# Fixing GpSimd's order in an attention layer, and moving the steps that scale its weights

## The chip, the cores and the metric

The kernel runs on one core of a Trainium2 chip. The metric is the device time of one execution, in microseconds. TensorE multiplies, VectorE and ScalarE work element by element and move results out of TensorE's accumulators (PSUM), GpSimd works element by element on SBUF, and SyncE issues the DMAs. Each engine takes its instructions in one fixed order, which is decided when the program is compiled.

## The reference, cut to what matters

A trunk of two layers runs over 512 prompt rows and 32 sample rows (544 columns here, since the kernel holds activations transposed). Layer 0 mixes tokens with an RWKV-7 recurrence. Layer 1, the only one that the change touches, is differential attention. Its input projection is one wide product:

```
h = rmsnorm(x, norm_w)
q, k, v, qm, gate = jnp.split(h @ w_in, [MIX_W, 2 * MIX_W, 3 * MIX_W, 3 * MIX_W + MEM_W], axis=-1)
...
attn = probs(q1, k1) - lam * probs(q2, k2)
o = rmsnorm(jnp.einsum('bhqk,bkhd->bqhd', attn, v), subln) * (1.0 - lam_init)
out = jnp.concatenate([o, mem_attention(qm, mk, mv)], axis=-1) * jax.nn.silu(gate)
return x + out @ w_out, k, v
```

There are 12 heads of width 128, four heads of attention to a memory of 256 rows, and a gate of 2048 columns. All is in float32, so the kernel makes each large product from parts.

## The kernel before, in words

**Blocks.** Layer 1's input projection is cut into 56 blocks of 128 output columns: for each head its values, keys and queries, then gates, and for four heads a memory query and a memory gate. `steps` (line 461) multiplies one block: two halves of 272 columns, eight contraction tiles in each, three matmuls to a tile, so 48 matmuls or steps, numbered 0 to 47. The three matmuls are high weight times high activation, high weight times low activation, and low weight times high activation. The first use of a block's low part is therefore its third matmul (step 2), and of the second half of that low part its fifteenth (step 14). After each half an evacuation moves the result out of PSUM: one ScalarE instruction for values, keys and memory queries, ScalarE and then VectorE for gates, and for queries two ScalarE and two VectorE instructions that take turns.

**Preparing a block's weights.** Raw weights are float32 and come by DMA into one of four buffers (`load_pair`, line 316; tile `h16s` in the profile). They are split into two float16 parts. First a power of two is found that brings them into float16's range: ScalarE squares all 1024 elements of a partition and adds them up (`square_total`, line 326; the squares themselves are thrown away into a tile `junkw`); TensorE adds the partitions with a matrix of ones (`total_spread`, line 336, a matmul with one column); VectorE makes the scale from the sum (`scales`, two small instructions). Then `split_scaled` (line 366) makes the parts, in halves of 512 elements: ScalarE writes the high part `whs` (raw times scale, rounded), GpSimd multiplies raw by the scale in place (line 374), GpSimd subtracts the high part and writes the low part `wls` (line 375). A last small GpSimd instruction (`inverse`, line 346, and for memory queries a second one) makes the inverse scale, with which the evacuation multiplies.

**Buffers.** `whs` has two buffers. `wls` has two buffers as well, under the tag "wlo", and from the fourth block on the discarded squares `junkw` take one of the same two (line 333). Which tile gets which buffer is decided by the compiler, in an order that it works out beforehand; a tile's buffer is free again when the last instruction that uses the tile is done.

**The order around the change.** `stream` (line 1879) runs the 56 blocks and places the preparation between matmuls. During block b it issues the split of block b+1 at the steps of SPLITS1 (two for `whs`, two for the scaling, two for the subtraction, one for the inverse), the load of block b+4 at the steps of LOADS1 (1 and 14), the squares of block b+3 at step 10 (STAT1), their sum over partitions at step 46 (SPREAD1, into a spare column of the second half's PSUM bank) and the scale in the next block at step 8 (SCALE1). `diff_layer` (line 1939) adds the attention of earlier heads at written-out places between the same matmuls: scores, exponentials, transposes, stores, weighted sums, memory attention.

**Queues.** In this stage TensorE, VectorE, ScalarE and SyncE are wrapped in `Queue` (line 124): while `self.ordered` is set, each instruction is tied behind the one issued before it on its engine, so that the order written in the code is the order that runs. GpSimd is not wrapped: its instructions are issued through `nc.gpsimd`, and the compiler chooses their order. The inverse is one that it moves: written as the last of the split, it runs right after the VectorE instruction that makes its scale. GpSimd's other work in this stage is the low part of the keys (`keys`, line 2010, two instructions per head) and one small product per gate (line 1993).

Of the kernel before, what the change touches and what calls it, by code (L numbers as in the profile page):

```python
# [18 lines left out]
P = 128  # L19
# [20 lines left out]
TILES1 = ((156,178),(188,210),(220,244),(254,280))  # L40
MEMAT1 = (60, 80, 180, 276, 294, 306, 324, 330, 346, 362, 402, 420, 484, 552)
MEMAT1B = MEMAT1[:10] + (400, 430, 490, 590)
LOADS1, SPLITS1 = (1, 14), (2, 5, 9, 13, 17, 20, 23)
STAT1, SPREAD1, SCALE1 = 10, 46, 8
EXP = float(1 << 23)
ROOT = float(0x5F3759DF) + 14 * EXP
SAMPLE1 = ((310, "s"), (338, "m"), (362, "t"), (386, "w"), (406, "n"), (464, "r"))
# [87 lines left out]
class Trunk:  # L135
# [187 lines left out]
            self.se.dma_start(raw[:, q * h : q * h + h], src[q * h * P : (q + 1) * h * P, c0 : c0 + P].rearrange("(k p) c -> p k c", p=P))  # L323
            yield

    def square_total(self, rec):

        rec["st"] = st = self.sts[rec["n"] % 4]
        with self.nc.allow_low_precision("a bound, rounded before a power of two is taken from it"):
            if rec["n"] < 3:  # L330
                junk = self.raws[3].bitcast(BF16)[:, :, :P]
            else:
                junk = self.wp.tile([P, KT, P], BF16, tag="wlo", name="junkw", bufs=2)[:]
            self.ae.activation(junk, rec["raw"], AF.Square, accum_out=st)

    def total_spread(self, rec, out, start):

        rec["sum"] = out
        self.te.matmul(out, self.ones16, rec["st"], start=start, stop=True, skip_group_check=not start)

    def scales(self, rec):

        rec["s"] = self.scale[:, rec["n"] : rec["n"] + 1]
        self.power(rec["s"], rec["sum"])

    def inverse(self, inv, rec):

        gp, kind = self.nc.gpsimd, rec["kind"]
        gp.tensor_scalar(inv.bitcast(I32), rec["s"].bitcast(I32), -1.0, self.cx[:, kind % 4 : kind % 4 + 1], ALU.mult, ALU.add)
        if kind == 4:  # L350
            gp.tensor_scalar(inv, inv, P ** -0.5, None, ALU.mult)

    def power(self, s, total):

# [3 lines left out]
    def measured(self, rec):  # L358

        if "s" not in rec:  # L360
            self.square_total(rec)
            ps = self.psx.tile([P, 512], F32, tag="x", name="ps_st")
            self.total_spread(rec, ps[:, 0:1], True)
            self.scales(rec)

    def split_scaled(self, rec):

        hi = self.wp.tile([P, KT, P], F16, tag="whi", name="whs", bufs=2)
        lo = self.wp.tile([P, KT, P], F16, tag="wlo", name="wls", bufs=2)
        raw, s = rec["raw"], rec["s"]  # L370
        ks = [slice(q * KT // 2, (q + 1) * KT // 2) for q in range(2)]
        gp = self.nc.gpsimd
        todo = [(lambda k=k: self.ae.activation(hi[:, k], raw[:, k], AF.Copy, scale=s), 0.0) for k in ks]
        todo += [(lambda k=k: gp.tensor_scalar(raw[:, k], raw[:, k], s, 1.0, ALU.mult, ALU.mult), 0.0) for k in ks]  # L374
        todo += [(lambda k=k: gp.tensor_tensor(lo[:, k], raw[:, k], hi[:, k], ALU.subtract), 0.0) for k in ks]  # L375
        inv = self.unscale[:, rec["n"] : rec["n"] + 1]
        todo.append((lambda: self.inverse(inv, rec), 0.0))
        return (hi, lo, inv), todo

    def weights(self, src, c0):  # L380

# [19 lines left out]
    def split(self, raw):  # L401

        if isinstance(raw, dict):
            return self.split_scaled(raw)
        third = self.third is not None and self.turn % 3 == 2
        self.turn += 1
        p, n = (self.third, 1) if third else (self.wp, 2)
        hi = p.tile([P, KT, P], F32R, tag="whi", name="whi", bufs=n)
        lo = p.tile([P, KT, P], F32R, tag="wlo", name="wlo", bufs=n)
        todo = []  # L410
        for q in range(2):
            k = slice(q * KT // 2, (q + 1) * KT // 2)
            todo.append((lambda k=k, q=q: self.ae.copy(hi[:, k], raw[q][:]), 0.0))
            low = self.nc.gpsimd if self.inner else self.ve
            todo.append((lambda k=k, q=q: low.tensor_tensor(lo[:, k], raw[q][:], hi[:, k].bitcast(F32), ALU.subtract), LATER))
        return (hi, lo), todo

# [43 lines left out]
    def steps(self, w, evac):  # L461

        n = 0
        for v in (slice(0, TH), slice(TH, T)):
            if len(self.open) > 1:
                self.until(self.open.pop(0))
            ps = self.psg.tile([P, 512], F32, tag="g", name="ps_g")
            for k in range(KT):
                for t, x in ((0, self.hh), (0, self.hl), (1, self.hh)):
                    self.te.matmul(ps[:, :TH], w[t][:, k, :], x[:, k, v], start=k == 0 and x is self.hh and t == 0,  # L470
                                             stop=k == KT - 1 and t == 1)
                    if k == KT - 1 and t == 1:
                        self.open.append(evac(ps[:, :TH], v))
                    yield
                    n += 1
                    if n == SPREAD1 and self.rec is not None:
                        self.total_spread(self.rec, ps[:, 2 * TH - 64 : 2 * TH - 63], False)

    @staticmethod
    def two(ap):  # L480
# [1269 lines left out]
    def scaled_pool(self):  # L1750

        nc, p = self.nc, self.h0
        self.hh, self.hl = (lambda t: (t[:, 0], t[:, 1]))(p.tile([P, 2, KT, T], F16, tag="hh", name="h16"))
        part = p.tile([P, KT * T], F32, tag="hl", name="h16s")
        self.raws = [part[:, i * D : i * D + D].rearrange("p (k c) -> p k c", c=P) for i in range(4)]
        at = 4 * D

        def small(n):
            nonlocal at
            at += n  # L1760
            return part[:, at - n : at]

        self.scale, self.unscale, self.ones16 = small(56), small(56), small(P // 2).bitcast(BF16)
        nc.gpsimd.memset(self.ones16, 1.0)
        self.sts = [small(1).bitcast(BF16)[:, 0:1] for _ in range(4)]
        self.subg = small(DH)
        self.nscaled = 0
        sq, st, sx, self.nwx, self.cx = small(KT), small(1).bitcast(BF16)[:, 0:1], small(1), small(KT), small(4)
        with nc.allow_low_precision("a bound, rounded before a power of two is taken from it"):
            self.ae.activation(sq, self.nw[1], AF.Square, accum_out=st)  # L1770
        ps = self.psx.tile([P, 512], F32, tag="x", name="ps_nw")
        self.te.matmul(ps[:, 0:1], self.ones16, st, start=True, stop=True)
        self.power(sx, ps[:, 0:1])
        self.ve.tensor_scalar(sx, sx, 2.0 ** -4, None, ALU.mult)
        self.ve.tensor_scalar(self.nwx, self.nw[1], sx, None, ALU.mult)
        for n in range(4):
            self.ve.tensor_scalar(self.cx[:, n : n + 1], sx.bitcast(I32), -1.0, (381.0 - n) * EXP, ALU.mult, ALU.add)
# [101 lines left out]
    def stream(self, makes):  # L1879
# [3 lines left out]
                return self.made.pop(0), []  # L1883
            return self.split(self.early.pop(0))

        cur = nxt()
        for make in makes:
            w, todo = cur
            for fn, _ in todo:
                fn()  # L1890
            cur = nxt()
            todo = cur[1]
            last = self.rec
            self.rec = next((x for x in self.early if isinstance(x, dict) and "st" not in x), None)
            raws = self.load_steps(*self.ahead.pop(0)) if len(self.early) < (3 if isinstance(self.early[0], dict) else 2) else iter(())
            for i, _ in enumerate(make(w)):
                yield
                if i in LOADS1:
                    next(raws, None)
                if i in SPLITS1 and todo:  # L1900
                    todo.pop(0)[0]()
                if i == SCALE1 and last is not None:
                    self.scales(last)
                if i == STAT1 and self.rec is not None:
                    self.square_total(self.rec)
        for fn, _ in cur[1]:
            fn()
        self.made.append(cur[0])
# [30 lines left out]
    def diff_layer(self, dq, p, mp, mctx, pool_early, order, made):  # L1939
# [50 lines left out]
        def make_gate(g):  # L1990
            def make(w):
                half[g] = w[2]
                nc.gpsimd.tensor_scalar(subg[:, g : g + 1], self.subs, w[2], None, ALU.mult)
                yield from self.steps(w, self.gate_evac(self.o1[g], w[2])[2])
            return make

# [13 lines left out]
        def keys(st):  # L2010
            k, h = st["k"], st["h"]
            st["kh"] = kh = dq.tile([P, 2, T], F32R, tag="kh", name="kh", bufs=QB)
            for m in range(2):
                hi = kh[rows[m], m, :]
                self.ae.copy(hi, k[rows[m], :])
                nc.gpsimd.tensor_tensor(self.kz[h % 2][rows[m], m, :], k[rows[m], :], hi.bitcast(F32), ALU.subtract)
            self.ae.copy(st["G"]["ks"][:, st["j"], :], k[:, TP:])
            st["kout"] = turn_out(k, 0, st["G"]["scr"][0][:, st["j"], :])

# [325 lines left out]
    def run(self):  # L2345
# [7 lines left out]
        self.ordered, self.later, self.open = False, [], []  # L2353
        self.place_no = self.acted = 0
        nc = self.nc
        self.te, self.ve, self.ae, self.se = (Queue(self, e) for e in (nc.tensor, nc.vector, nc.scalar, nc.sync))
        self.c = self.pool("const", 1)
        self.hctx = ExitStack()
        hp = self.pool("h", 1, ctx=self.hctx, side="right")
# [60 lines left out]
```

## Time and profile before

| what | value |
|---|---|
| median of the runs | 1400.07 us |
| runs | 1396.4, 1400.07, 1400.42 us |
| profiled execution, its own time | 1406.7 us |
| its span, from first to last instruction | 1404.5 us |
| attention layer's 56 blocks, first matmul to end | 826.8 to 1275.2 us of the span |

The profile is of one execution. A row of a group gives the line of the code (132 is the line of the helper that issues all queued instructions), the engine, the operation, what it writes and reads, the shape and the count; then the busy time, the mean duration in ns, and the time that the engine stood idle just before, with what ended it. In the timeline the columns are start, duration, and the same names; the bracket at the end is the idle time before and its releaser, where "issue" stands for a wait that the profile could not put down to one. PEld is TensorE's weight load, a suffix q (POOLq, SPq) an engine's sequencer.

### The profile page before, as it was taken

How to read it: one execution, taken by the hardware profiler on the slowest of the kernel's cores; microseconds unless marked ns; L12 is line 12 of the kernel's file. 1: busy time of each engine (PE TensorE's matmuls, PEld its weight loads, DVE VectorE, ACT ScalarE, POOL GpSimd, SP SyncE). 2: the span in 40 equal slices, each digit the busy share in tenths (PEclk: the TensorE clock that was granted, in tenths of full speed). 3: DMA queues.
4: the chain of work that ended last, by engine and by line, in shares of the span. 5: the costliest groups of instructions: out<-in, count | busy, mean ns of one | idle time of the engine just before them, and what ended most of it. 6: DMA issues, size and time to landing. Idle time of an engine off the chain costs nothing. (4 is left out here: it accounts for less than half of the span.)

```text
span 1404.5 us, 31863 instructions
## 1 busy us (share of the span) xinstructions
PE 1315.7 (94%) x11657; PEld 1197.3 (85%) x11657; DVE 907.9 (65%) x2319; ACT 852.7 (61%) x2204; POOL 646.2 (46%) x1175
## 2 busy tenths in 40 slices
PE   6999999999999999899999999989999898999797
PEld 6998899999999999898899987868777776778797
DVE  7766777788778777766763545545774567756343
ACT  7665677777776777565553357656655675763221
POOL 2227576556755585620120077555554655561000
PEclk9999999999999999999999999999999999999898
DMA  7552223332233323333384447756776667666421
GB/s 241 177 137 56 61 55 93 84 76 68 73 84 79 77 62 80 79 86 121 108 258 127 130 128 170 155 142 160 170 167 132 154 139 179 147 155 194 148 68 64
DMA packets 418295, 171.51 MB, mean 122 GB/s; under 512 B 195210, under 2 KB 402579, under 8 KB 418139
## 3 DMA queue, kind: packets, MB, share of 16 engines
q1 hardware_dynamic: 417994, 168.96, 46.5%
q8 instruction: 92, 1.51, 0.5%
q14 instruction: 65, 0.52, 0.1%
q10 hardware_dynamic: 144, 0.52, 0.1%
HBM read 130.84 MB, written 41.92 MB: 123 GB/s over the span
## 5 line engine op out<-in xcount | busy, mean ns | idle before, releaser
L132 PE MATMUL ps_g<-h,whs 128*128 128x272 f16 x1792 | 329.1, 283 | 0.0
L132 PE MATMUL ps_g<-hl,whi 128*128 128x272 f32 x976 | 284.3, 297 | 0.6 <-POOL hl L581 0.5
L132 PE MATMUL ps_g<-hh,wlo 128*128 128x272 f32 x912 | 277.6, 304 | 1.3 <-DVE wlo L132 1.3
L132 PE MATMUL ps_g<-hh,whi 128*128 128x272 f32 x912 | 275.0, 302 | 0.9 <-ACT hh L132 0.9
L132 PE MATMUL ps_g<-h,wls 128*128 128x272 f16 x896 | 254.1, 284 | 17.8 <-POOL wls L375 17.7
L870 POOL TENSOR_TENSOR tm<-u,m 102x84 f32<-102x84 f32 (+23 forms) x372 | 158.1, 425 | 166.1 <-DMA m<-sc 138.0
L132 PEld LDWEIGHTS <-whs 128*128 128x128 f16 x1792 | 176.5, 99 | 38.6 <-issue 4.8
L132 DVE TENSOR_TENSOR wlo<-raw,whi 128x512 fp32r<-128x512 f32 x208 | 148.7, 730 | 83.7 <-ACT whi L132 82.4
L132 PEld LDWEIGHTS ps_g<-hl,whi 128*128 128x128 f32 x976 | 184.1, 191 | 2.4 <-POOL hl L581 0.7
L132 ACT CAST whi<-raw 128x512 fp32r<-128x512 f32 x210 | 125.3, 616 | 98.1 <-PE ps_g L132 44.5
L132 PEld LDWEIGHTS ps_g<-hh,whi 128*128 128x128 f32 x912 | 174.7, 192 | 4.4 <-ACT hh L132 1.3
L132 PEld LDWEIGHTS ps_g<-hh,wlo 128*128 128x128 f32 x912 | 174.2, 191 | 4.8 <-DVE wlo L132 2.1
L872 POOL TENSOR_TENSOR u<-u,tm 102x84 f32<-102x84 f32 (+23 forms) x372 | 159.1, 428 | 29.1
L132 PE MATMUL ps_g<-hi,whi 128*128 128x272 f32 x448 | 130.7, 292 | 11.0 <-ACT hi L132 11.0
L375 POOL TENSOR_TENSOR wls<-h16s,whs 128x512 f16<-128x512 f32 x112 | 128.1, 1164 | 18.7 <-issue 9.8
L132 PE MATMUL ps_g<-lo,whi 128*128 128x272 f32 x448 | 130.9, 292 | 0.9 <-DVE lo L132 0.9
L132 PE MATMUL ps_g<-hi,wlo 128*128 128x272 f32 x448 | 130.3, 291 | 0.2 <-DVE wlo L132 0.2
L132 PEld LDWEIGHTS <-wls 128*128 128x128 f16 x896 | 88.7, 99 | 41.4 <-POOL wls L375 21.6
L374 POOL TENSOR_SCALAR h16s<-h16s 128x512 f32<-128x512 f32 x112 | 78.9, 714 | 50.9 <-ACT whs L132 49.6
L132 PEld LDWEIGHTS ps_g<-hi,whi 128*128 128x128 f32 x448 | 85.6, 191 | 11.3 <-ACT hi L132 11.2
L132 PEld LDWEIGHTS ps_g<-lo,whi 128*128 128x128 f32 x448 | 85.5, 191 | 1.8 <-DVE lo L132 1.8
L132 PEld LDWEIGHTS ps_g<-hi,wlo 128*128 128x128 f32 x448 | 85.7, 191 | 0.4 <-DVE wlo L132 0.4
(423 smaller groups left out, 2941.2 us busy)
## 6 DMA issues: line engine op xcount, KB each, us to landing
raw<-in_rw_in_dram SPq DMA_DIRECT2D x114, 256.0 KB
h16s<-in_df_in_dram SPq DMA_DIRECT2D x112, 256.0 KB
raw<-in_w_out_dram SPq DMA_DIRECT2D x64, 256.0 KB
ptr<-pk SPq DMA_DIRECT2D x44, 160.0 KB
aT<-ptr SPq DMA_DIRECT2D x11, 640.0 KB
scr<-sg SPq DMA_DIRECT2D x96, 68.0 KB
out_dram<-scr SPq DMA_DIRECT2D x6, 1024.0 KB
m<-sc SPq DMA_DIRECT2D x36, 128.0 KB
```

The costliest lines, as they stand in the source:

```text
L132: return lambda *a, **k: self.trunk.tie(self, issue(*a, **k))
L374: todo += [(lambda k=k: gp.tensor_scalar(raw[:, k], raw[:, k], s, 1.0, ALU.mult, ALU.mult), 0.0) for k in ks]
L375: todo += [(lambda k=k: gp.tensor_tensor(lo[:, k], raw[:, k], hi[:, k], ALU.subtract), 0.0) for k in ks]
L870: nc.gpsimd.tensor_tensor(tm[:, :n, :wd], u3[:, :n, kx : kx + 1].to_broadcast(sh), m3[:, kx : kx + 1, kx + 1 :].to_broadcast(sh), ALU.mult)
L872: nc.gpsimd.tensor_tensor(u3[:, :n, kx + 1 :], u3[:, :n, kx + 1 :], tm[:, :n, :wd], ALU.add)
```

## The change

GpSimd gets a `Queue` of its own (`self.ge`) and the attention layer's GpSimd instructions go through it. The inverse scale is made by VectorE, right behind the scale, and so is the product per gate. The squares are made in two halves of 512 elements, at steps 11 and 27, each with its own sum; the discarded tile is taken at the first half and dropped after the second. The sum over partitions (now two matmuls, one for each half's sum, accumulating in one column) moves to step 12 of the next block, and scale and inverse to step 20 there. The split's places move from steps 2, 5, 9, 13, 17, 20 to 2, 5, 7, 9, 12, 15; its seventh place, the inverse's, is gone.

```diff
-LOADS1, SPLITS1 = (1, 14), (2, 5, 9, 13, 17, 20, 23)
-STAT1, SPREAD1, SCALE1 = 10, 46, 8
+LOADS1, SPLITS1 = (1, 14), (2, 5, 7, 9, 12, 15)
+STAT1, SPREAD1, SCALE1 = (11, 27), 12, 20
...
-    def square_total(self, rec):
-
-        rec["st"] = st = self.sts[rec["n"] % 4]
+    def square_total(self, rec, q):
+
+        if q == 0:
+            rec["st"] = self.sts[rec["n"] % 4]
+            if rec["n"] < 3:
+                rec["junk"] = self.raws[3].bitcast(BF16)[:, :, :P]
+            else:
+                rec["junk"] = self.wp.tile([P, KT, P], BF16, tag="wlo", name="junkw", bufs=2)[:]
+        k = slice(q * KT // 2, (q + 1) * KT // 2)
         with self.nc.allow_low_precision("a bound, rounded before a power of two is taken from it"):
-            if rec["n"] < 3:
-                junk = self.raws[3].bitcast(BF16)[:, :, :P]
-            else:
-                junk = self.wp.tile([P, KT, P], BF16, tag="wlo", name="junkw", bufs=2)[:]
-            self.ae.activation(junk, rec["raw"], AF.Square, accum_out=st)
+            self.ae.activation(rec["junk"][:, k], rec["raw"][:, k], AF.Square, accum_out=rec["st"][:, q : q + 1])
+        if q:
+            del rec["junk"]
 
     def total_spread(self, rec, out, start):
 
         rec["sum"] = out
-        self.te.matmul(out, self.ones16, rec["st"], start=start, stop=True, skip_group_check=not start)
+        for q in range(2):
+            self.te.matmul(out, self.ones16, rec["st"][:, q : q + 1], start=start and q == 0, stop=True,
+                           skip_group_check=not (start and q == 0))
 
     def scales(self, rec):
 
-        rec["s"] = self.scale[:, rec["n"] : rec["n"] + 1]
-        self.power(rec["s"], rec["sum"])
-
-    def inverse(self, inv, rec):
-
-        gp, kind = self.nc.gpsimd, rec["kind"]
-        gp.tensor_scalar(inv.bitcast(I32), rec["s"].bitcast(I32), -1.0, self.cx[:, kind % 4 : kind % 4 + 1], ALU.mult, ALU.add)
+        rec["s"], rec["inv"] = (t[:, rec["n"] : rec["n"] + 1] for t in (self.scale, self.unscale))
+        self.power(rec["s"], rec.pop("sum"))
+        kind, inv = rec["kind"], rec["inv"]
+        self.ve.tensor_scalar(inv.bitcast(I32), rec["s"].bitcast(I32), -1.0, self.cx[:, kind % 4 : kind % 4 + 1], ALU.mult, ALU.add)
         if kind == 4:
-            gp.tensor_scalar(inv, inv, P ** -0.5, None, ALU.mult)
+            self.ve.tensor_scalar(inv, inv, P ** -0.5, None, ALU.mult)
...
-        gp = self.nc.gpsimd
+        gp = self.ge
...
-        inv = self.unscale[:, rec["n"] : rec["n"] + 1]
-        todo.append((lambda: self.inverse(inv, rec), 0.0))
-        return (hi, lo, inv), todo
+        return (hi, lo, rec["inv"]), todo
...
                     if n == SPREAD1 and self.rec is not None:
-                        self.total_spread(self.rec, ps[:, 2 * TH - 64 : 2 * TH - 63], False)
+                        self.total_spread(self.rec, ps[:, 480:481], False)
...
-        cur = nxt()
+        cur, rec = nxt(), None
...
-            last = self.rec
-            self.rec = next((x for x in self.early if isinstance(x, dict) and "st" not in x), None)
+            self.rec, rec = rec, next((x for x in self.early if isinstance(x, dict) and "st" not in x), None)
...
-                if i == SCALE1 and last is not None:
-                    self.scales(last)
-                if i == STAT1 and self.rec is not None:
-                    self.square_total(self.rec)
+                if i == SCALE1 and self.rec is not None:
+                    self.scales(self.rec)
+                if i in STAT1 and rec is not None:
+                    self.square_total(rec, STAT1.index(i))
...
-                nc.gpsimd.tensor_scalar(subg[:, g : g + 1], self.subs, w[2], None, ALU.mult)
+                self.ve.tensor_scalar(subg[:, g : g + 1], self.subs, w[2], None, ALU.mult)
...
-                nc.gpsimd.tensor_tensor(self.kz[h % 2][rows[m], m, :], k[rows[m], :], hi.bitcast(F32), ALU.subtract)
+                self.ge.tensor_tensor(self.kz[h % 2][rows[m], m, :], k[rows[m], :], hi.bitcast(F32), ALU.subtract)
...
-        self.te, self.ve, self.ae, self.se = (Queue(self, e) for e in (nc.tensor, nc.vector, nc.scalar, nc.sync))
+        self.te, self.ve, self.ae, self.se, self.ge = (Queue(self, e) for e in (nc.tensor, nc.vector, nc.scalar, nc.sync, nc.gpsimd))
```

More of the change, by code (lines that the diff above doesn't have):

```diff
@@ L360, in measured @@
         if "s" not in rec:
-            self.square_total(rec)
+            for q in range(2):
+                self.square_total(rec, q)
             ps = self.psx.tile([P, 512], F32, tag="x", name="ps_st")
@@ L413, in split @@
             todo.append((lambda k=k, q=q: self.ae.copy(hi[:, k], raw[q][:]), 0.0))
-            low = self.nc.gpsimd if self.inner else self.ve
+            low = self.ge if self.inner else self.ve
             todo.append((lambda k=k, q=q: low.tensor_tensor(lo[:, k], raw[q][:], hi[:, k].bitcast(F32), ALU.subtract), LATER))
@@ L1764, in scaled_pool @@
         nc.gpsimd.memset(self.ones16, 1.0)
-        self.sts = [small(1).bitcast(BF16)[:, 0:1] for _ in range(4)]
+        self.sts = [small(1).bitcast(BF16) for _ in range(4)]
         self.subg = small(DH)
```

## The prediction

> **What bounds the kernel now.** The page's header and its busy times came first, then the windows of the attention layer's 56 blocks (columns: us, busy time of PE, PEld, DVE, ACT and POOL, granted clock, DMA share, GB/s).
>
> ```profile
> span 1404.5 us, 31863 instructions
> PE 1315.7 (94%) x11657; PEld 1197.3 (85%) x11657; DVE 907.9 (65%) x2319; ACT 852.7 (61%) x2204; POOL 646.2 (46%) x1175
> 826.80:1275.20 448.40, 413.83 (x3451) 341.07 (x3449) 271.04 (x780) 286.25 (x689) 264.65 (x326) 0.97 0.66 151
> ```
>
> TensorE bounds the kernel, and also this stage: 413.83 of 448.40 us, where VectorE, ScalarE and GpSimd have 271, 286 and 265. Some 35 us at most are idle time of TensorE here. So small work on the other three costs nothing by itself; what counts is which wait TensorE meets. Next, therefore, the waits of PE in this stretch (total us, how often, longest), and the line that most of them name, seen from GpSimd:
>
> ```profile
> PE ps_g L132 <- POOL wls L375: 17.7, 12, 2.9
> PE ps_s L132 <- ACT pt L132: 12.1, 5, 4.6
> PE ps_g L132 <- ACT junkw L132: 2.0, 1, 2.0
> L375 POOL TENSOR_TENSOR wls<-h16s,whs x112: 1144/1156/1607, 828.9 to 1260.8; 128x512 f16<-128x512 f32 x112
> L375 POOLq EVENT_SEMAPHORE  x56: 17/994/2697, 827.1 to 1257.5; - x56
> ```
>
> The largest wait is for the low part `wls`: 17.7 us. But the last row is odd: ahead of the subtractions, GpSimd's sequencer stands at a semaphore in every block, median 994 ns, though GpSimd is busy only 59% of the stage. The timeline shows for what. Block 7, on ACT, POOL and PE:
>
> ```profile
> 880.21 1.06 ACT L132 ACTIVATE junkw<-h16s 128x1024 bf16<-128x1024 f32 x1 [1.18 <-DMA h16s<-in_df_in_dram]
> 881.17 0.19 ACT L132 ACTIVATION_READ_ACCUMULATOR junkw<-h16s 128x1 bf16 x1
> 881.95 0.48 ACT L132 ACTIVATE og<-ps_g,h16s 128x272 f32<-128x272 f32 x1
> 878.54 1.36 POOL L374 TENSOR_SCALAR h16s<-h16s 128x512 f32<-128x512 f32 x2
> 881.50 2.27 POOL L375 TENSOR_TENSOR wls<-h16s,whs 128x512 f16<-128x512 f32 x2 [1.60 <-issue]
> 883.30 0.39 PE L132 MATMUL ps_g<-h,whs 128*128 128x272 f16 x2
> 883.53 0.28 PE L132 MATMUL ps_g<-h,wls 128*128 128x272 f16 x1
> 1160.91 0.19 ACT L132 ACTIVATION_READ_ACCUMULATOR junkw<-h16s 128x1 bf16 x1
> 1161.24 2.28 POOL L375 TENSOR_TENSOR wls<-h16s,whs 128x512 f16<-128x512 f32 x2 [2.00 <-issue]
> ```
>
> Raw and `whs` are ready and the scaling ends at 879.90. The subtraction still stands for 1.60 us and starts 0.14 us after the square's accumulator was read (881.17+0.19=881.36). At 1161.24 it is the same: 0.14 us behind the square. In 31 of the 53 blocks that have such a square the subtraction starts 0.08 to 0.14 us behind it. The subtraction reads nothing that the square writes. What they share is the tag "wlo" with its two buffers: one holds the block that TensorE is reading, the squares take the other, and only when they are thrown away does the next `wls` get it. This hold is what the forecast turns on. Today it mostly costs nothing: block 8 needs its `wls` at 883.53, and the first half is there at 881.50+1.16=882.66, 0.87 us early.
>
> **The squares in two halves.** Today the hold lasts one instruction of 1046 ns and a read of 192 ns, placed at step 10. After, the tile is taken at step 11 and kept until the second half at step 27. That half stands on ScalarE behind the evacuation of step 24.
>
> ```profile
> L132 ACT ACTIVATE junkw<-h16s 128x1024 bf16<-128x1024 f32 x53 | 55.5, 1046 | 6.8 <-DMA h16s<-in_df_in_dram 4.5 <-PE ps_g L132 2.3
> L132 ACT ACTIVATION_READ_ACCUMULATOR junkw<-h16s 128x1 bf16 x53 | 10.2, 192 | 0.0
> L132 ACT ACTIVATE whs<-h16s 128x512 f16<-128x512 f32 x110 | 73.4, 714 | 1.2 <-PE ps_g L132 1.2
> ```
>
> A half has no row. A ScalarE instruction on 512 elements takes 714 ns; with its read, which overlaps it by 0.1 (880.21+1.06 against 881.17), that is 0.71+0.19-0.10=0.81 us. Bounds: 0.62 us (half of 1046 plus a read that overlaps as now) and 0.91 (no overlap). ScalarE's added work is 2x0.81-1.15=0.47 us a block, 25 us in all; it hides in the 162 us that ScalarE is idle here, except where the evacuation waits behind it.
>
> In block 7 the evacuation ends at 881.95+0.48=882.43; its present start is that of a matmul, not of ScalarE, so it stays. Second half square: to about 883.14 at the least bound, 883.24 at 0.81, and a little earlier where ScalarE pipelines the two; I take 883.14. Subtraction from 883.28, first half there at 884.44, needed at 883.53 less the 0.06 us that TensorE takes to start behind GpSimd: a new wait of 0.97 us. In short, the hold ends 1.8 us later than now, 0.87 of which the block has to spare.
>
> The earlier places of the subtraction (12 and 15 for 17 and 20) don't help: it didn't stand for its place, but for the buffer. I did this block's sum for each of the 53, with its own evacuation and its own time to spare. Twenty blocks get no wait, 16 one of up to 1.1 us, 17 a longer one: 45.6 us. There is a second way out of the hold: TensorE's reading of the other buffer ends with the block. Then the wait is the same in each block: 0.14+1.16+0.06 behind the block's last matmul, less the 0.23 from its first matmul to the low part's (883.30 to 883.53), 1.1 us; 53 of them are 58 us. Where each block takes the earlier of both ways, the sum is 27.5 us. So 27.5 to 58, and I take 0.8 us a block, 42 us, nearest to the first way: it follows the present rows, where a square is released to the next subtraction. The 17.7 us of today are within these sums and go: +24.3.
>
> **GpSimd in program order, without inverses.** An inverse is 263 ns, for memory queries and gate products 288; VectorE takes 154 ns for the like.
>
> ```profile
> L349 POOL TENSOR_SCALAR h16s<-h16s 128x1 int32<-128x1 int32 x54 | 14.2, 263 | 80.6 <-DVE h16s L132 35.2 <-DVE ps_s L132 35.1 <-DVE srs L132 6.7
> L1993 POOL TENSOR_SCALAR h16s<-dv,h16s 128x1 f32<-128x1 f32 x12 | 3.5, 288 | 1.0
> L132 DVE TENSOR_SCALAR h16s<-h16s 128x1 int32<-128x1 int32 x53 | 8.2, 154 | 1.8
> 951.87 0.26 POOL L349 TENSOR_SCALAR h16s<-h16s 128x1 int32<-128x1 int32 x1
> 952.21 1.34 POOL L2016 TENSOR_TENSOR kz<-k,kh 64x544 fp32r<-64x544 f32 x1
> 953.64 0.21 POOL L351 TENSOR_SCALAR h16s<-h16s 128x1 f32<-128x1 f32 x1
> 953.93 1.36 POOL L374 TENSOR_SCALAR h16s<-h16s 128x512 f32<-128x512 f32 x2
> 955.26 2.27 POOL L375 TENSOR_TENSOR wls<-h16s,whs 128x512 f16<-128x512 f32 x2
> 956.47 0.29 PE L132 MATMUL ps_g<-h,wls 128*128 128x272 f16 x1 [1.39 <-POOL wls L375]
> ```
>
> VectorE gets some 70 of them, 70x0.154=11 us, behind 177 us of idle time: nothing. Fixing the order moves no other step, since GpSimd runs in the written order already but for the inverses. What they are worth shows in the rows from 951.87: a query block, where keys, scaling and subtraction run without a gap and TensorE waits 1.39 us behind them. Out of this chain fall 0.34 us (951.87 to 952.21) and 0.29 (953.64 to 953.93): 0.63 us. In twelve heads that would be 12x0.63=7.6 us of the 17.7. With the hold longer, the subtraction in these blocks waits for the square instead, which the sum above holds already; so I book nothing.
>
> **Spread and scale in the next block.** Sum at step 12 instead of 46: the wait for the square, 2.0 us once, goes. A block has one more matmul with one column:
>
> ```profile
> 882.93 0.28 PE L132 MATMUL ps_g<-h,whs 128*128 128x272 f16 x1
> 883.05 0.17 PE L132 MATMUL ps_g<-h16s 128*128 128x1 bf16 x1
> 883.07 0.28 PE L132 MATMUL ps_g<-h,whs 128*128 128x272 f16 x1
> ```
>
> The two big ones stand 0.14 us apart with it, otherwise 0.116 (5.6 us by 48): 0.03 us, 53x0.03=1.5 us. Even 0.1 would be 5.3. Scale and inverse at step 20 rather than 8 still stand 30 steps, over 3 us, ahead of the first use at step 2 of the following block: nothing.
>
> **What is late next.** The raw buffer is reloaded when the subtraction has read it. On SyncE's queue the loads, and every store and load issued behind them, wait for it:
>
> ```profile
> SPq L132 <- POOL wls L375: 85.4, 38, 6.8
> DVE to L132 <- DMA mspread<-to: 17.3, 4, 6.7
> 876.82 0.29 PE L132 MATMUL ps_g<-h,wls 128*128 128x272 f16 x1 [1.50 <-POOL wls L375]
> 1034.90 0.41 PE L132 MATMUL ps_g<-h,wls 128*128 128x272 f16 x1 [2.60 <-POOL wls L375]
> 872.00:882.00 10.00, 8.50 (x76) 7.08 (x74) 2.87 (x10) 7.00 (x18) 7.61 (x12) 1.00 0.89 186
> 1030.00:1040.00 10.00, 7.40 (x52) 5.96 (x51) 8.37 (x21) 4.20 (x10) 6.10 (x9) 0.83 0.86 175
> ```
>
> Loads come 1 to 2 us later; squares wait for DMA 4.5 us today, so 0 to 5 us more, of which I take none on the path. Against that, TensorE's 12.1 us for `pt`, which go back to VectorE's waits for a DMA, partly run out behind the new waits: 0 to 9, I take -3.
>
> The clock: the wait of 1.50 us at 876.82 left it at 1.00, that of 2.60 at 1034.90 comes with 0.83 and a matmul of 0.41. In the block sums three waits exceed 2.6 us; at 0.17x10 us each that is 5 us, kept for the upper end. The Trainium skill ("TensorE: Matmul & The Clock Gate", Part 1) has the clock halved only after an idle window of about 3.4 us. By that rule nothing but one wait of 5 us would cost clock; the row at 1034.90 shows that a shorter one comes with a lower mean clock already.
>
> Sum: +24.3-2.0+1.5-3 = +21 us. The profiled execution of 1406.7 us (span 1404.5) becomes 1428; it is 6.6 above the median of 1400.07, so I give 1421.
>
> **The rivals.** 0.3%, 4.2 us, is about what a measurement of this kernel can tell from no change.
>
> *A, faster:* the subtraction isn't held by the second half, because the compiler gives it the buffer first or lets squares and low parts each keep one. Then GpSimd's relief counts: -7.6-2.0+1.5 = -8, 1392; with a part of the 12.1 us it is 1388. For it: the subtraction is written before step 27, and buffers are the compiler's choice. Against: the 31 blocks in which the square went first although it was not needed. Decided by whether a subtraction starts before the second half-square of its block ends.
>
> *B, slower by more:* only the squares release, the later loads make squares wait for DMA, which lengthens the hold again, and the waits of over 2.6 us take clock: 45.6 to 58, less 17.7, +5 for clock, +5 for DMA less 2.0, plus 1.5: +37 to +50, about 1440. For it: the 85.4 us of SyncE behind this very line. Against: squares wait for DMA only 4.5 us in 53 today.
>
> *C, the same:* each block takes the earlier way out: 27.5-17.7-2.0+1.5 = +9, and the 12.1 us for `pt` absorb it: 1400. Against: nothing reclaims these waits in every head.
>
> **How the numbers follow.** Forecast 0.55, A 0.20, B 0.15, C 0.10. Forecast and B are slower: 0.70; C the same: 0.10; A faster: 0.20. The likeliest's own range goes from 27.5 to 50 us of waits, 1406 to 1429. The range to state cuts half of A and some of B: 1396 to 1444.
>
> **What would show it.** Right: the waits of PE for `wls` L375 at 35 to 50 us in 30 or more rows; L375 starting about 0.14 us behind the second half-square, with GpSimd's idle time before it, over 2 us in many blocks; the row for `junkw` gone from PE's waits; half-squares of 0.6 to 0.75 us. Wrong: L375 running at its new places, next to the scaling, with the 17.7 us falling to about 10 (A); or waits of nearly one size, 1.1 us, at each block's start (second way); or new rows of ScalarE waiting for DMA or for `wls` (B).

## The result, and the profile after

| | before | after |
|---|---|---|
| median of the runs | 1400.24 us (4 runs) | 1440.13 us (1434.65 to 1442.5, 4 runs) |
| ratio | | 1.0283, 95% interval 1.0246 to 1.0320 |
| profiled execution, own time | 1406.7 us | 1434.65 us |
| its span | 1404.5 us | 1432.9 us |
| attention layer's 56 blocks | 826.8 to 1275.2 us | 825.3 to 1305.8 us |

The kernel became slower, by 40 us against 21 forecast. The profile's header and TensorE's row, and the window of the 56 blocks (columns as before):

```profile
span 1432.9 us, 32093 instructions
PE 1319.4 (92%) x11713; PEld 1193.0 (83%) x11713; DVE 918.0 (64%) x2391; ACT 865.7 (60%) x2316; POOL 627.2 (44%) x1103
825.30:1305.80 480.50, 417.70 (x3506) 336.61 (x3504) 278.26 (x849) 299.89 (x796) 245.73 (x254) 0.99 0.61 141
```

The stage is 480.5 us long instead of 448.4. TensorE's busy time hardly differs, so the new time is idle time of TensorE: 62.8 us for 34.6. What ended it, in the same stretch:

```profile
PE ps_g L132 <- DVE h16s L132: 35.6, 52, 4.1
PE ps_g L132 <- POOL wls L132: 27.0, 27, 1.7
```

The second row is the wait of the prediction, at 27.0 us for 17.7. The first is one that the prediction did not have: in 52 blocks a matmul waits for VectorE, which is writing into `h16s`, the scale. The rows of before for `pt` (12.1) and `junkw` (2.0) are gone. These four add up to +35.6+9.3-12.1-2.0 = 30.8 us; the span grew by 28.4. The medians stand 40 us apart: the profiled execution of before is 6.5 us above its median, that of after 5.5 below its own, so the rows account for the 28 alone.

**The new wait, in one block.** The timeline, PE, then DVE, then PE:

```profile
886.67 0.28 PE L132 MATMUL ps_g<-h,wls 128*128 128x272 f16 x1
886.99 0.16 DVE L132 TENSOR_SCALAR h16s<-ps_g 128x1 int32<-128x1 int32 x1 [0.89 <-PE ps_g L132]
887.20 0.39 PE L132 MATMUL ps_g<-h,whs 128*128 128x272 f16 x2 [0.25 <-DVE h16s L132]
```

The matmul of step 20 ends at 886.95. VectorE, which reads the sum out of the spare column, starts 0.04 us later, having waited 0.89 us for "PE ps_g", though the sum was made nine block matmuls earlier (at 885.70). TensorE's step 21 starts 0.05 us after VectorE is done. So VectorE's read is fenced on both sides: it waits for the last matmul into this PSUM tile, and the next matmul into it waits for the read. From 886.67 to 887.20 is 0.53 us where 0.12 is usual: 0.41 us, the smallest such loss in any of the 52; 0.25 us of it is idle time, which is what the row counts.

In 25 of the 52 blocks this is all: VectorE stands ready, and the 25 waits are 6.2 us together. In the other 27 VectorE comes late, out of other work (16 times out of the reduction that makes `snm`), and TensorE waits for that too: 29.3 us. The longest, on DVE and PE:

```profile
1193.13 0.45 DVE L132 STREAM_TRANSPOSE pk<-pt 128x256 f32<-128x256 f32 x1
1193.49 0.12 DVE L132 TENSOR_SCALAR h16s<-ps_g 128x1 int32<-128x1 int32 x1
1193.67 0.61 PE L132 MATMUL ps_g<-h,whs 128*128 128x272 f16 x2 [4.08 <-DVE h16s L132]
```

Without the fence, VectorE's lateness at this place would not be TensorE's (experiment 12). In the kernel before the sum was made at step 46 of one block and read at step 8 of the next, when TensorE was writing another tile.

**The hold.** ACT, then POOL and PE, in a query block:

```profile
874.02 0.63 ACT L132 ACTIVATE junkw<-h16s 128x512 bf16<-128x512 f32 x1
874.55 0.19 ACT L132 ACTIVATION_READ_ACCUMULATOR junkw<-h16s 128x1 bf16 x1
874.88 2.27 POOL L132 TENSOR_TENSOR wls<-h16s,whs 128x512 f16<-128x512 f32 x2 [0.78 <-POOL h16s L132]
876.09 0.29 PE L132 MATMUL ps_g<-h,wls 128*128 128x272 f16 x1 [1.21 <-POOL wls L132]
```

The subtraction starts 0.14 us behind the second half-square's read (874.74), as forecast; TensorE waits 1.21 us. Two blocks on, it starts behind TensorE instead:

```profile
890.93 0.28 PE L132 MATMUL ps_g<-h,wls 128*128 128x272 f16 x1
891.36 2.27 POOL L132 TENSOR_TENSOR wls<-h16s,whs 128x512 f16<-128x512 f32 x2 [4.44 <-PE ps_g L132]
892.57 0.29 PE L132 MATMUL ps_g<-h,wls 128*128 128x272 f16 x1 [1.14 <-POOL wls L132]
```

The first row is the last matmul of its block; it ends at 891.21, and 0.15 us later GpSimd starts, after 4.44 us of standing. The addresses in the compiled programs agree: before, no block's low part has the buffer of the block ahead of it; after, 17 of 56 have it. In the trace these 17 start about 0.15 us behind TensorE, and 35 more start 0.14 or 0.15 us behind a second half-square. The 17 cost TensorE 1.13 us each, 19.2 of the 27.0 us; the 35 cost 6.0 us, in nine blocks.

### The profile page after: what moved, and what is told of

It reads as the page before. It is cut to its first block, busy times and chain, and to the rows that moved or that the text cites. A ratio compares the mean times of both kernels' runs of the same rounds, so it can differ in the third digit from the quotient of the medians.

```text
span 1432.9 us, 32093 instructions
## 1 busy us (share of the span) xinstructions
PE 1319.4 (92%) x11713; PEld 1193.0 (83%) x11713; DVE 918.0 (64%) x2391; ACT 865.7 (60%) x2316; POOL 627.2 (44%) x1103
## 5 line engine op out<-in xcount | busy, mean ns | idle before, releaser
L132 PE MATMUL ps_g<-h,whs 128*128 128x272 f16 x1792 | 327.3, 280 | 35.6 <-DVE h16s L132 35.6
L132 PEld LDWEIGHTS <-whs 128*128 128x128 f16 x1792 | 171.4, 98 | 75.4 <-issue 46.1
L872 POOL TENSOR_TENSOR tm<-u,m 102x84 f32<-102x84 f32 (+23 forms) x372 | 152.9, 411 | 163.9 <-DMA m<-sc 135.9
L874 POOL TENSOR_TENSOR u<-u,tm 102x84 f32<-102x84 f32 (+23 forms) x372 | 164.2, 441 | 29.1
```

The lines of the kernel that those rows point to most:

```text
L132: return lambda *a, **k: self.trunk.tie(self, issue(*a, **k))
L872: nc.gpsimd.tensor_tensor(tm[:, :n, :wd], u3[:, :n, kx : kx + 1].to_broadcast(sh), m3[:, kx : kx + 1, kx + 1 :].to_broadcast(sh), ALU.mult)
L874: nc.gpsimd.tensor_tensor(u3[:, :n, kx + 1 :], u3[:, :n, kx + 1 :], tm[:, :n, :wd], ALU.add)
```

## The experiments

The theory after the comparison: two costs, a *read fence* (the sum stands in the tile that TensorE is still writing) and the *hold* (squares keep the shared buffer from step 11 to 27). The main rivals: the first wait is only a late VectorE, or it covers time that would be lost to the low part anyway. Times are given as the ratio to the kernel before, run on the same chip, with its 95% interval; 0.0010 is 1.4 us.

### 1. Scale read after the tile is done

```
-STAT1, SPREAD1, SCALE1 = (11, 27), 12, 20
+STAT1, SPREAD1, SCALE1 = (11, 27), 12, 24
```

> One number differs from the changed kernel: the scale is made at step 24, in the second half of the block, instead of step 20; all else as changed. Theory 1 (read fence): VectorE's read of the sum at step 20 stands between TensorE's steps 20 and 21, which write the same PSUM tile, and TensorE waits for it: 35.6 us in 52 waits in the profile of the changed kernel. After step 23 no matmul writes that tile any more, so the 35.6 us go; part of TensorE's waits for pt (12.1 us before, none after) come back: 1402 to 1417 us, and no row of PE waiting for DVE h16s. Rival 2 (VectorE is simply late with the scale, or these waits only cover a later release of the low part): the wait for DVE h16s becomes a longer one for wls, and the time stays at 1430 to 1442 us.

1.0156 (1.0129 to 1.0183), 1422.78 us. PE's waits:

```profile
PE ps_g L132 <- POOL wls L132: 41.5, 36, 1.7
PE ps_s L132 <- ACT pt L132: 7.0, 3, 3.2
PE ps_oT L132 <- DVE ot L132: 4.6, 2, 4.2
```

No row for DVE h16s is left, so the wait comes from VectorE's read at that place. Of the 41.5 us, 26 are now of subtractions behind TensorE (23 blocks) and 12 of subtractions behind a square. But the time, 18 us better than the changed kernel, misses both ranges. The rows say why: waits for `wls` go from 27.0 to 41.5, `pt` comes back with 7.0 and `ot` with 4.6, so that 26 of the 35.6 us only change their name. That leaves about 10; the two profiled executions (1434.65 and 1421.14) are 13.5 us apart. So each theory was partly right: the fence is real, and 14.5 us of it, four tenths, lay over the hold.

### 2. Squares in a buffer of their own

```
-                rec["junk"] = self.wp.tile([P, KT, P], BF16, tag="wlo", name="junkw", bufs=2)[:]
+                rec["junk"] = self.wp.tile([P, KT, P], BF16, tag="raw", name="junkw", bufs=RAWS)[:]
```

> The changed kernel with the discarded squares in a buffer of their own (one of the raw-weight buffers of layer 0, idle in this stage), scale still at step 20. Theory 1: the hold of the shared buffer costs the 27.0 us that TensorE waits for wls, 27 times; some 8 to 10 us of it are GpSimd's chain in the query blocks and stay: 1420 to 1425 us, with the 35.6 us for DVE h16s unchanged, and L132 subtractions following the scaling at once. Rival 2 (the low part is late because GpSimd or ScalarE is late, not because of the buffer): wls waits stay at 20 us or more and the time stays at 1434 to 1442 us.

1.0109 (1.0086 to 1.0132), 1416.22 us. PE's waits, and GpSimd in one block:

```profile
PE ps_g L132 <- DVE h16s L132: 39.4, 52, 5.1
PE ps_g L132 <- POOL wls L132: 4.9, 8, 1.7
```

```profile
879.28 1.36 POOL L132 TENSOR_SCALAR h16s<-h16s 128x512 f32<-128x512 f32 x2 [1.52 <-ACT whs L132]
880.60 2.27 POOL L132 TENSOR_TENSOR wls<-h16s,whs 128x512 f16<-128x512 f32 x2
```

The subtraction now follows the scaling without a gap, and 22 of the 27.0 us go. That is more than expected: the fence, which stays, leaves GpSimd more time in the query blocks too. Experiment 3, without it, has 11.6 us there.

### 3. Both

Edits 1 and 2 together.

> Both repairs in the changed kernel: scale at step 24 and squares in a buffer of their own. Theory 1, the two costs add: 1440 - 35.6 - 18 = 1386 us, plus up to 9 us of returning waits for pt: 1386 to 1395 us, faster than the kernel before. Rival 2 (one cost hides behind the other): 1402 to 1417 us, no better than the scale alone.

0.9964 (0.9946 to 0.9982), 1397.25 us: faster than the kernel before, and 2 us above the theory's range.

```profile
PE ps_g L132 <- POOL wls L132: 11.6, 11, 2.7
PE ps_s L132 <- ACT pt L132: 10.2, 5, 3.2
```

Against the changed kernel that is -3.1%, about 45 us, where the two repairs alone gave 18 and 24. The two costs nearly add (42 of 45 us), and together they are all of the slowdown and a little more.

### 4. The kernel before, squares in a buffer of their own

> The kernel before with only the discarded squares moved to a buffer of their own. Theory 1 with the prediction's reading: before the change the hold mostly ran out in spare time, so it costs only the waits of the blocks in which the square released late, about 2 to 6 us: 1394 to 1400 us, while GpSimd's idle time labelled issue (up to 2 us a block) goes. Rival 3 (the 17.7 us of waiting for wls before were the hold): about 1383 us.

0.9962 (0.9946 to 0.9979), 1396.76 us, within the range. Waits for `wls` and `ot`, and GpSimd's sequencer ahead of the subtractions:

```profile
PE ps_g L132 <- POOL wls L375: 8.2, 9, 3.1
PE ps_oT L132 <- DVE ot L132: 2.6, 2, 2.1
L375 POOLq EVENT_SEMAPHORE  x55: 17/17/17, 830.4 to 1248.5; - x55
```

The semaphore at which GpSimd stood for 994 ns in the median takes 17: that wait was the hold. The waits for `wls` fall by 9.5 us, the time by 5.3 (0.38%); the rest comes back in several small waits, the largest of them for `ot`. So in the old places the hold costs some 5 us, and in the new ones, without the fence, 27 (experiment 1 against 3: 1.0156 and 0.9964).

### 5. A second read of the sum

On edit 2, a power of two is taken from the sum at step 16 as well:

```
+                if i == 16 and self.rec is not None:
+                    self.power(self.scale[:, self.rec["n"] : self.rec["n"] + 1], self.rec["sum"])
```

> The changed kernel with squares in a buffer of their own (as in the second experiment, 1.1% over the kernel before), and the sum in PSUM read by VectorE at step 16 as well as at step 20, so that TensorE's steps are cut twice a block. Theory 1: a read between two matmuls of the same PSUM tile costs about 0.41 us where VectorE is free, so 52 more of them cost about what the first ones cost between the second and third experiment (19 us): ratio to before 1.020 to 1.030, and PE's waits for DVE h16s go from 39 to about 65 us or more. Rival 2 (the wait is for a late VectorE, not for the read as such): the first read takes up the wait and the second finds VectorE in time: ratio 1.008 to 1.014.

1.0315 (1.0277 to 1.0352), 1446.5 us.

```profile
PE ps_g L132 <- DVE h16s L132: 64.3, 104, 3.7
```

Twice as many waits, 104 for 52, and 24.9 us more of them: 0.48 us each. The time rose by 2.1%, 29 us, a little over the range. In 33 of the 52 second reads, 4 steps behind the first, VectorE is not late: it stands ready, and TensorE still waits 0.25 us. In the other 19, and in most of the first reads, it is late, so the rival's cause is there too; only with the fence does it reach TensorE.

### 6. Both halves early

```
-STAT1, SPREAD1, SCALE1 = (11, 27), 12, 20
+STAT1, SPREAD1, SCALE1 = (10, 11), 12, 24
```

> The changed kernel with the scale at step 24 and both half-squares at steps 10 and 11, in the shared buffer. Theory 1: it is the time of the hold that costs, not the sharing; ending the hold ahead of the evacuation at step 24 brings the waits for wls from 41.5 us (first experiment) down to 10 to 18 us: ratio to before 0.996 to 1.004. Rival 4 (two halves cost by their number, each with its read, on ScalarE): the ratio stays at 1.010 or more.

1.0077 (1.0050 to 1.0103), 1413.12 us: between the two ranges.

```profile
PE ps_g L132 <- POOL wls L132: 22.1, 19, 2.7
```

A shorter hold halves the waits (41.5 to 22.1), but does not bring them back to those of before. In 14 blocks the compiled program still gives the low part the buffer that TensorE is reading; 13 of these subtractions start right behind TensorE's last matmul, and TensorE waits 1.1 us for each, 14.5 of the 22 us. Why it chooses so here, and in no block of experiment 11 (one whole square at step 10, the subtraction at step 12 too), was not settled.

### 7. GpSimd's order and the inverses alone

The kernel before, with the queue for GpSimd and inverses and gate products on VectorE, and nothing else of the change.

> The kernel before with only GpSimd in program order and the inverses and gate products on VectorE; squares, spread, scale and split places as before. The prediction's rival A put GpSimd's relief at 0.63 us in each of twelve query blocks, 7.6 us at most: ratio 0.9945 to 0.998, with wls waits down from 17.7 to about 10 us. If the order has a price of its own that the other parts hid: 1.000 to 1.005.

0.9956 (0.9934 to 0.9978), 1394.4 us.

```profile
PE ps_g L132 <- POOL wls L132: 11.6, 12, 1.9
```

17.7 us become 11.6 and the time falls by 6.2: rival A's price of 7.6 us was near. This part of the change is a gain.

### 8. The same, and squares in a buffer of their own

> The kernel before with GpSimd in program order, inverses on VectorE, and the squares in a buffer of their own: the two parts that the runs so far put on the gaining side, without halves and without the moved spread. Theory 1: the waits for wls of 8.2 us (fourth experiment) fall to 1 to 4: ratio 0.990 to 0.995, the fastest of all. Rival: the query blocks' wait is for something later than GpSimd's chain and the ratio stays at 0.996, as in the fourth experiment.

0.9954 (0.9932 to 0.9976), 1394.45 us.

```profile
PE ps_g L132 <- POOL wls L132: 10.6, 11, 1.9
```

The two gains do not add: the ratio is the rival's, but not its reason. What is left stands, for the most part, behind GpSimd's own chain in the query blocks, where keys, scaling and subtraction run without a gap, whatever the buffer:

```profile
911.07 2.75 POOL L132 TENSOR_TENSOR kz<-k,kh 64x544 fp32r<-64x544 f32 x2 [2.28 <-ACT kh L132]
913.92 1.36 POOL L132 TENSOR_SCALAR h16s<-h16s 128x512 f32<-128x512 f32 x2
915.24 2.26 POOL L132 TENSOR_TENSOR wls<-h16s,whs 128x512 f16<-128x512 f32 x2
916.45 0.29 PE L132 MATMUL ps_g<-h,wls 128*128 128x272 f16 x1 [0.84 <-POOL wls L132]
```

### 9. A tile for each half-square

Edit 1, and the discarded tile taken at each half and dropped after it, so that nothing is held between steps 11 and 27.

> The first experiment's kernel (scale at step 24, shared buffer) with a discarded tile taken and dropped anew for each half-square, so that nothing is held between step 11 and step 27. In its compiled program both halves of a block still get the buffer that the next subtraction then takes, in 43 of 53 blocks, ahead of it. Theory 1 (the subtraction waits for the last square that uses its buffer, wherever the tile is dropped): little better than the first experiment, wls waits of 32 to 42 us, ratio to before 1.010 to 1.016. Rival 5 (it is the tile held over 16 steps that costs): wls waits below 20 us, ratio 1.000 to 1.006.

1.0081 (1.0054 to 1.0108), 1413.98 us, under the theory's range and over the rival's. My reading of the program's order in that expectation was wrong, as the timeline shows: the subtraction comes between the halves. PE's waits, then the end of a block on PE and ACT:

```profile
PE ps_g L132 <- POOL wls L132: 22.9, 16, 2.7
```

```profile
905.56 0.28 PE L132 MATMUL ps_g<-h,wls 128*128 128x272 f16 x1
905.93 0.63 ACT L132 ACTIVATE junkw<-h16s 128x512 bf16<-128x512 f32 x1 [1.16 <-POOL wls L132]
906.56 0.47 ACT L132 ACTIVATE v<-ps_g,h16s 128x272 f32<-128x272 f32 x1
```

Without the hold over 16 steps the waits go from 41.5 to 22.9 us, and the time falls by 10.5 of the 27 us that the hold costs at these places. But now the second half finds both buffers taken, one by the new low part and one by TensorE, and stands on ScalarE until the block ends (its last matmul ends at 905.84; the first half of the `wls` that the bracket names was done at 905.08), with the evacuation behind it. So it goes in 34 of the 53 blocks, for 58 us of ScalarE's time. Two buffers for three tiles are one too few, and part of the wait only changes its place.

### 10 and 11. The split's earlier places

Experiments 8 and 7, each with the places 7, 9, 12, 15 for scaling and subtraction.

> The eighth experiment (the kernel before, GpSimd in program order without inverses, squares in a buffer of their own) with the changed kernel's earlier places for scaling and subtraction (7, 9, 12, 15). Nothing holds the subtraction now but its place and its inputs. Theory 1: it runs as GpSimd comes free, and the 10.6 us that are left stand behind GpSimd's chain of keys, scaling and subtraction, which the places don't shorten: ratio 0.992 to 0.997, as in the eighth. Rival: the places were what held the low part, and wls waits fall under 4 us: 0.986 to 0.991.

> The seventh experiment (the kernel before, GpSimd in program order without inverses) with the earlier places, squares still in the shared buffer, whole, at step 10. Theory 1: the subtraction still stands behind the square, so the places are worth nothing: ratio 0.993 to 0.998, as in the seventh. If the compiler, seeing the subtraction earlier, gives it the buffer that TensorE reads in some blocks, waits of about 1.2 us each come in: 1.000 or more.

0.9981 (0.9965 to 0.9998) and 0.9986 (0.9968 to 1.0005). Waits for `wls`, in 10 and in 11:

```profile
PE ps_g L132 <- POOL wls L132: 10.6, 11, 1.9
```

```profile
PE ps_g L132 <- POOL wls L132: 10.6, 12, 1.8
```

The waits stay as they were, as forecast. But both ratios lie just above the ranges expected (up to 0.997 and 0.998), and above those of 8 and 7, with intervals that overlap: the places gain nothing, and a small loss stays open.

### 12. The sum in a PSUM tile of its own

Edit 2, and, with the read still at step 20:

```
-                        self.total_spread(self.rec, ps[:, 480:481], False)
+                        other = self.psg.tile([P, 512], F32, tag="g", name="ps_st")
+                        self.total_spread(self.rec, other[:, 480:481], True)
```

> The second experiment's kernel (squares in their own buffer, scale at step 20) with the sum over partitions in a PSUM tile of its own, taken from the three that the blocks' halves use in turn; VectorE's read stays at step 20. Theory 1, sharpened (the fence comes from the sum standing in the tile that TensorE is still writing): PE's waits for DVE h16s fall from 39.4 us to under 5, and the ratio to before to 0.995 to 1.003, near the third experiment, with a few us of waits for a free tile perhaps. Rival 6 (any read of PSUM by VectorE at step 20 stops TensorE there, whatever tile): the waits stay at 35 us or more and the ratio at 1.008 to 1.014.

0.9919 (0.9893 to 0.9944), 1390.19 us, the fastest of all and faster than the range expected.

```profile
PE ps_g L132 <- POOL wls L132: 12.8, 11, 1.8
PE ps_g L132 <- ACT qs L132: 7.7, 4, 3.2
PE ps_g L132 <- DVE h16s L132: 0.2, 1, 0.2
```

The window of the 56 blocks, in experiment 3 and in this one:

```profile
824.70:1263.90 439.20, 411.34 (x3504) 339.97 (x3504) 278.62 (x848) 296.14 (x793) 246.84 (x258) 0.98 0.67 154
```

```profile
822.40:1254.40 432.00, 406.52 (x3504) 336.86 (x3503) 281.91 (x846) 296.20 (x794) 248.27 (x259) 1.00 0.68 156
```

The same read at the same step, in another tile: 39.4 us of waits become 0.2. So it is the shared tile that fences, not VectorE's reading of PSUM. The 7.7 us for `qs` are waits of block matmuls for ScalarE's last evacuation of a query block, which the other kernels do not have; a tile fewer for the halves would explain them, but this was not tried by itself. It beats experiment 3 by 0.45%. The windows differ by 7.2 us; 4.8 of them are TensorE's busy time for the same number of matmuls, at a granted clock of 1.00 for 0.98. Why the waits for `pt`, 10.2 us there, are 0.8 here was not tried.

## Why the prediction was right in its sign and short in its size

**The hold: right as a cause; that its size came out where it stood alone is partly luck.** The forecast was 42 us of waits for `wls`. Without the fence there are 41.5 (experiment 1). In the changed kernel 27.0 were left, in 27 rows instead of 30 or more, because the fence delays TensorE by 35.6 us in the same blocks, and a delayed TensorE needs its low part later. Both ways out occur, 35 and 17 times; which of them is no race on the chip but fixed in the compiled program by the buffer that a tile gets. That is why "earliest of both", 27.5 us, was not the rule that I took it for: its near agreement with 27.0 is chance, as experiment 1 shows. The 42 us were taken as nearest to the first way, the square's release, which alone was to give 45.6; in experiment 1 that way gives 12 us and the second, TensorE's, 26.

**Spread and scale in the next block: the step that failed.** The prediction booked one more matmul, 1.5 us, and "scale and inverse at step 20 ... nothing", since only their distance from the first use was asked. It did not ask what the PSUM tile of the sum is doing at step 20. That cost 35.6 us of waits and, net of what they covered, 18 us: about what the forecast lacked (1440 against 1421). The kernel before could have warned: the sum was read there in step 8 of the next block, and no row showed a read from a tile in the middle of its matmuls. That 1440 still lies in the stated range is luck: the likeliest case's own range ended at 1429, and what lies above it stood there for rival B.

The Trainium skill ("PSUM — Partial Sum Buffer", PSUM bank collisions raise a hardware error) has the rule: two engines may not touch the same bank in the same 32 partitions at once, even in other columns, and the compiler's back end orders any two such instructions. By that rule, a read at step 20 waits for step 20's matmul and step 21 waits for the read; the traces agree: 0.41 us or more in each of 52 blocks, 0.2 us in all when the sum has another tile. It names the bank where the runs tell tiles apart; here a tile is a whole bank's 512 columns, so no run separates the two.

**The inverses: right to book nothing here.** Freed GpSimd is worth 6 us by itself (experiment 7); in the changed kernel it shows nowhere, since the subtraction waits for a buffer.

**What is late next: half right.** A half-square with its read was sized at 0.81 us. In block 7's sum it is 0.71 (882.43 to 883.14), which the prediction calls the least bound; but the bound of 0.62 ends at 883.05, and 0.71 is an instruction without its read. Measured it is 0.72 (874.02 to 874.74), so this choice came out by luck. The rows:

```profile
L132 ACT ACTIVATE junkw<-h16s 128x512 bf16<-128x512 f32 x106 | 66.0, 622 | 2.6 <-PE ps_g L132 2.4
L132 ACT ACTIVATION_READ_ACCUMULATOR junkw<-h16s 128x1 bf16 x106 | 20.7, 195 | 0.0
SPq L132 <- POOL wls L132: 142.9, 45, 7.8
```

SyncE's queue stands behind the subtraction for 142.9 us instead of 85.4, as expected, but no square waits for a load (the 4.5 us of before are gone, since the halves come later), so rival B's chain did not form. Nor did the clock fall: 0.99 in the stage after 0.97. No wait for `wls` is over 1.7 us, but those at the fence reach 4.1, and the 10 us from the end of that one show 0.86. And the 12.1 us for `pt` ran out entirely where 3 were taken.

## What to carry to other kernels

Before moving a small read or write of PSUM to another step, ask which matmuls go into that tile around it: each read between them cost 0.41 us or more here, the more the later VectorE came, and next to nothing when the tile was done or another one. When a scratch tile shares buffers with a tile on the critical path, count how long it is held, and look at GpSimd's idle time before the instruction that needs the buffer: it showed the hold before the change, when it cost little. Two waits in the same stretch cover each other, so a wait's row is not what its repair gives: taking away 35.6 us of one gave 18, because 14.5 us of the other came up from under it, and 11 of two more.

## What the runs showed that I had not expected

A VectorE instruction of 0.16 us on 128 elements stopped TensorE for 0.41 us: 0.16 us until the last matmul is through, 0.04 until VectorE starts, 0.16, and 0.05 until TensorE goes on. That is the price where VectorE stands ready. Where it came out of other work, TensorE waited up to 4.1 us for the same small read: a read that costs little by itself made the lateness of another engine TensorE's own.
